# Modulation closes in three spaced calls under the down projections, and four whole tiles in place of five in the first FFN

## Chip, core and metric

The kernel runs on one core of one Trainium2 chip. The metric is the device time of one execution in microseconds (us); the time before is the median of three runs. Traces come from one profiled execution. Engines are TensorE (PE, its weight loads PEld), VectorE (DVE), ScalarE (ACT), GpSimd (POOL) and SyncE (SP, which only issues transfers).

## What is computed

One layer of a diffusion backbone: 512 latent tokens (LAT) and 256 context tokens (CX), width 1024, FFN width 2816 = 22 tiles of 128.

```python
ml = split(silu(c)     @ w_mod + b_mod, 9)      # nine modulation vectors of 1024, latent
mc = split(silu(c_ctx) @ w_mod + b_mod, 9)      # the same for the context tokens
lat += 0.5 * ml[2] * swiglu(modulate(rms_norm(lat, g0), ml[0], ml[1]), w_gu[0], w_down[0])
cx  += 0.5 * mc[2] * swiglu(modulate(rms_norm(cx,  g0), mc[0], mc[1]), w_gu[0], w_down[0])
h_lat, h_ctx = modulate(rms_norm(lat, g1), ml[3], ml[4]), modulate(rms_norm(cx, g1), mc[3], mc[4])
lat += ml[5] * merge(diff_attn(h_lat, h_ctx), pool_mix(h_lat))
lat += 0.5 * ml[8] * swiglu(modulate(rms_norm(lat, g2), ml[6], ml[7]), w_gu[1], w_down[1])
out = rms_norm(lat, g_final)
```

Everything is float32. A product of two float32 matrices is made of three TensorE matmuls on split operands (`mm3`, L141: hi*hi, lo*hi, hi*lo).

## The kernel before

**Order.** The program is written in one order; a planner that estimates times puts each engine's instructions into a queue of its own, which the chip then runs strictly in that order. `tc.issue_after(x)` keeps an instruction behind `x` in the queue of the engine that both share.

**First FFN, up and gate.** The 768 tokens are two streams of 384. The first five of the 22 tiles (`PLAIN1 = 5`) are whole tiles (`Hidden`, L373): gate and up, 8 k-tiles, two streams, 3 matmuls each = 96 matmuls of 384 columns. The other 17 are made by `Quad` (L426): seven products of 4 k-tiles from sums of weight and activation halves, 7 x 4 x 3 = 84 matmuls of 384 columns, for which DVE, ACT and POOL form and split more operands. The sums of activation halves (`HalfSums.build`, L514, four of them) are put behind the products of the third, fourth and fifth whole tile (L709 to L716). A quad's weights are prepared one quad ahead. Results go to DRAM (`store_act`, L656).

**First FFN, down.** The stored tiles come back (`Stored`, L533: a transfer, two ACT copies, two DVE subtractions) in chunks of 2, 5, 8, 3 and 4 (`ACT_CHUNKS`). A chunk is eight groups `i` of `ffn_down` (L549), each n x 6 matmuls and an update of `xo` and `xc` (L571) on DVE. The tiles of the next chunk are loaded meanwhile. The last chunk runs three times: context tokens (weight parts on POOL), then two halves of the latent tokens, with norms between its groups.

**Modulations 2 to 8** (`Mod`, L239) are work that runs beside this. A modulation has eight steps (L245: a 512 KB transfer issued by POOL into `wm`, then one DVE instruction on `macc` for each stream; 2 to 4 have two streams, 5 to 8 one) and a close: `total` (L257: TensorE matmuls that add `macc` over the partitions, L263, then an ACT copy, L266) and `finish` (L268: four small matmuls on that copy, L272, and one DVE addition, L275). Modulations 0 and 1 are made at the start in another way. Modulations 2, 3, 4 hang on the quads: each quad after the first calls `next_pending` twice (L489, L494). Modulations 5 to 8 hang on the down groups: `MOD_STEPS` says how many items each group of chunks 0 to 3 takes (L802). In the list `pending` (L724) a close is two more items behind the eight steps, so a call that takes three items can hold the last step, `total` and `finish` together. What is left runs behind chunk 3 (L804), then `scale_vec(7)` and `gate_vec(8)`.

Of the kernel before, what the change touches and what calls it, by code (L numbers as in the profile page):

```python
# [17 lines left out]
AF = mybir.ActivationFunctionType  # L18
# [6 lines left out]
KT = D // P  # L25
SEQ = 512
CTX = 256
# [8 lines left out]
CHUNKS = (4, 4, 4, 4, 2, 4)  # L36
ACT_CHUNKS = (2, 5, 8, 3, 4)

MOD_STEPS = (0, 1, 3, 2)

PLAIN1 = 5

PLAIN = 4
PARTS = 4
# [58 lines left out]
def tile_layer(ctx: ExitStack, tc: tile.TileContext, a: dict, out: bass.AP):  # L103
    nc = tc.nc
# [8 lines left out]
    latest = {}  # L113
    dr = ctx.enter_context(tc.tile_pool(name="dr", bufs=1, space=bass.MemoryType.DRAM))

    LAT, CX = 0, 1
# [13 lines left out]
    def weights(src, lo_engine=None):  # L130

        _, k, n = src.shape
        raw = wts.tile([P, 1024], F32, name="w_raw", bufs=3)
        hi = wts.tile([P, 1024], F32R, name="w_hi")
        lo = wts.tile([P, 1024], F32R, name="w_lo")
        v = lambda t: t[:, 0:k * n].rearrange("p (k n) -> p k n", n=n)
        nc.sync.dma_start(out=v(raw), in_=src)
        split(hi[:, 0:k * n], lo[:, 0:k * n], raw[:, 0:k * n], lo_engine)
        return v(hi), v(lo)

    def mm3(outs, wh, wl, acts, start, stop):  # L141

        for o, (ah, al) in zip(outs, acts):
            nc.tensor.matmul(out=o, lhsT=wh, rhs=ah, start=start, stop=False)  # L144
            nc.tensor.matmul(out=o, lhsT=wh, rhs=al, start=False, stop=False)  # L145
        for o, (ah, al) in zip(outs, acts):
            latest["pe"] = nc.tensor.matmul(out=o, lhsT=wl, rhs=ah, start=False, stop=stop)  # L147
        return sum(o.shape[-1] for o in outs) * 3 / 2400.0
# [23 lines left out]
    def bank(n=512):  # L172
        t = psum["ring"].tile([P, 512], F32, name="ps")
        return t[:, 0:n]

    def table(func, after):

        nc.scalar.activation(out=dummy, in_=after[:, 0:1], func=func, scale=0.0, bias=eps)
# [102 lines left out]
    def mod(i, kt, s):  # L281
        return mods[:, 8 * i + kt, s:s + 1]

    def scale_vec(i, norm, kts=range(KT), ns=2):

        n = len(kts)
        t = mods[:, 8 * i + kts[0]:8 * i + kts[0] + n, 0:ns]
        g = vecs[:, gn_col + 8 * norm + kts[0]:gn_col + 8 * norm + kts[0] + n]
        nc.vector.scalar_tensor_tensor(out=t, in0=t, scalar=1.0, in1=g.unsqueeze(2).broadcast_to([P, n, ns]),
                                       op0=ALU.add, op1=ALU.mult)  # L290

    def gate_vec(i, ns=2):

        t = mods[:, 8 * i:8 * i + 8, 0:ns]
        nc.vector.tensor_scalar(out=t, in0=t, scalar1=0.5, scalar2=None, op0=ALU.mult)
# [253 lines left out]
    def ffn_down(w_down, j0, acts, spans, after=no_after, held=None, lo_engine=None):  # L549

        n = len(acts)
        held = {} if held is None else held
        for i in range(KT):
            i0 = i - i % 2 if n <= 4 else i
            ws = slice((i - i0) * P, (i - i0 + 1) * P)
            if i0 not in held:
                cols = slice(0, 2 * P) if n <= 4 else slice(i % 2 * P, (i % 2 + 1) * P)  # L560
                held[i0] = weights(w_down[i0 // 2, 0, :, j0:j0 + n, cols], lo_engine)
            wh, wl = held[i0]
            outs = [bank(s[1]) for s in spans]
            for k in range(n):
                mm3(outs, wh[:, k, ws], wl[:, k, ws],
                    [acts[k].parts(o, m) if isinstance(acts[k], Stored) else
                     (acts[k].hi[:, o:o + m], acts[k].lo[:, o:o + m]) for o, m, *_ in spans],
                    k == 0, k == n - 1)
            for po, (o, m, xs, x0, gate_i, s) in zip(outs, spans):
                xa = xs[i][:, x0:x0 + m]  # L570
                latest["dve"] = nc.vector.scalar_tensor_tensor(out=xa, in0=po, scalar=mod(gate_i, i, s), in1=xa,  # L571
                                                               op0=ALU.mult, op1=ALU.add)
                after(i, s, x0, xa)
            yield i

    def run(gen, inserts=None):

        for i in gen:
            if inserts and i in inserts:
                inserts[i]()  # L580
# [34 lines left out]
    xc = [xc_all[:, k, :] for k in range(KT)]  # L615
# [34 lines left out]
    w_gu1, w_dn1 = a["gu"][0], a["dn"][0]  # L650
# [5 lines left out]
    def store_act(j, gate):  # L656
        nc.gpsimd.dma_start(out=act_dram[j], in_=gate)

    first = [Hidden(w_gu1, j, None, both, store_act) for j in range(PLAIN1)]
    early = [(first[0], 0), (first[0], 1), (first[1], 0)]  # L660
# [38 lines left out]
    sums1 = HalfSums(hb, HALF, tq1, row, nc.vector)  # L699
    quads1 = {j: Quad(w_gu1, j, wq1, 2, cq1, sums1, row, lambda q, gate: store_act(q.j, gate)) for j in range(PLAIN1, NJ)}  # L700
    for j, qd in quads1.items():
# [13 lines left out]
                    sums1.build(k)  # L715
        h_.close()  # L716

    pending = []
    behind = {}

    def add_mods(idx, pool_):
        for i in idx:
            m = Mod(i, pool_, (LAT, CX) if i < 5 else (LAT,))
            pending.extend([lambda m=m, kt=kt: m.step(kt) for kt in range(KT)] + [m.total, m.finish])  # L724

    def next_pending(n=1):

        for _ in range(min(n, len(pending))):
            with ExitStack() as order:
                for ins in (behind.get("dve"), latest["pe"]):  # L730
                    if ins is not None:
                        order.enter_context(tc.issue_after(ins.ins))
                pending.pop(0)()
        behind["dve"] = latest["dve"]

    add_mods((2, 3, 4), modp1)
    stored = []
    for j, qd in quads1.items():
        qd.all(next_pending if j > PLAIN1 else None)
        if not pending and not stored:  # L740
            right_stack.close()
            act_a = pool("act_a", right_stack, bufs=ACT_CHUNKS[0], side="right")
            raw_a = pool("raw_a", right_stack, bufs=1, side="right")
            for n in range(ACT_CHUNKS[0]):
                t = act_a.tile([P, 2, ALL], F32R, name="act_a")
                stored.append(Stored(act_dram[n], raw_a, t[:, :, 0:SEQ], t[:, :, SEQ:ALL]))
# [10 lines left out]
    def stream_tile():  # L757
        t = xo.tile([P, KT, SEQ], F32, name="xo")
        return t, [t[:, k, :] for k in range(KT)]
# [5 lines left out]
    xc = [xc_all[:, k, :] for k in range(KT)]  # L765
# [4 lines left out]
    rawp = pool("rawp", ffn_stack, bufs=2)  # L770
    modp = pool("modp", ffn_stack, bufs=2)
    add_mods((5, 6, 7, 8), modp)
    hctx_stack = ExitStack()
    HCW = CTX + 8
# [4 lines left out]
    def bring(j0, n, own):  # L779

        got = []
        for k in range(n):
            if own:
                t = actp.tile([P, 2, ALL], F32R, name="act")
                lt, ct = t[:, :, 0:SEQ], t[:, :, SEQ:ALL]
            else:
                lt = hp.tile([P, 2, SEQ], F32R, name=f"hl{k}")
                ct = hcp.tile([P, 2, HCW], F32R, name=f"hc{k}")[:, :, 0:CTX]
            got.append(Stored(act_dram[j0 + k], rawp, lt, ct))
        return got  # L790
# [3 lines left out]
    acts = stored  # L794
    for c, n in enumerate(ACT_CHUNKS[:-1]):
        nj = ACT_CHUNKS[c + 1]
        if c == 1:

            right_stack.close()
            hcp = pool("hcp", hctx_stack, bufs=1, side="right")  # L800
        following = bring(starts[c + 1], nj, c + 1 != 2)
        run(ffn_down(w_dn1, starts[c], acts, every), {i: lambda c=c: next_pending(MOD_STEPS[c]) for i in range(KT)})  # L802
        acts = following
    while pending:  # L804
        next_pending()
    scale_vec(7, 2, ns=1)
    gate_vec(8, 1)
    nc.sync.dma_start(out=edge, in_=a["edge"])
    lambdas()
    hl, hc = hl_new(), hc_new()  # L810
    st, held, j0 = Stats(), {}, starts[-1]
    run(ffn_down(w_dn1, j0, acts, [(SEQ, CTX, xc, 0, 2, CX)], st, held, nc.gpsimd), {1: lambda: table(AF.Sqrt, st.acc[CX, 0])})
    run(ffn_down(w_dn1, j0, acts, [(0, 256, xl, 0, 2, LAT)], st, held),
        Norm(st.acc[CX, 0], xc, 0, CX, 4, 3, hc).inserts(1))
    run(ffn_down(w_dn1, j0, acts, [(256, 256, xl, 256, 2, LAT)], st, held),
# [109 lines left out]
    _, o_raw = stream_tile()  # L925
# [271 lines left out]
    st = Stats()  # L1197
# [165 lines left out]
```

## Time and profile before

| | us |
|---|---|
| median of three runs | 1470.77 (1470.31 to 1474.37) |
| the profiled execution | 1472.54 |
| its span, first to last instruction | 1470.7 |
| TensorE busy | 1423.0 (97%) |
| VectorE busy | 1083.2 (74%) |
| ScalarE busy | 643.6 (44%) |
| GpSimd busy | 407.4 (28%) |

The span is cut by the program into: start and whole tiles (0 to about 117 us), quads (to about 370), down projection of the first FFN (to about 580), attention (to about 915), merge and second FFN. A line number in a row is that of the helper that issues the instruction. "PEclk" is the granted TensorE clock as a share of 2.4 GHz; 0.50 is 1.2 GHz.

### The profile page before, as it was taken

The page shows a single profiled execution, that of the slowest core. Times are in us where ns is not written, and L with a number is a line of the kernel's source. Part 1 is how long each engine was busy: PE and PEld are TensorE (multiplying, and loading weights), DVE is VectorE, ACT ScalarE, POOL GpSimd, SP SyncE. Part 2 cuts the span into 40 slices and gives each one's busy share as a digit, 9 for nine tenths or more (in the row PEclk, how much of TensorE's full clock was granted, in tenths as well). Part 3 has the DMA queues.
Part 4 walks back from the last instruction along what each step waited for, and adds up shares of the span by engine and source line. Part 5 has one row for each costly group of instructions (what it writes and reads, how often), then busy time and mean ns, then how long its engine had stood idle before and what let it go on. Part 6 is the DMA issues. An engine that isn't in the chain of part 4 may idle for free.

```text
span 1470.7 us, 22771 instructions
## 1 busy us (share of the span) xinstructions
PE 1423.0 (97%) x9076; PEld 1312.0 (89%) x9076; DVE 1083.2 (74%) x1613; ACT 643.6 (44%) x1034; POOL 407.4 (28%) x319
## 2 busy tenths in 40 slices
PE   6999999999989989989999999999999999999997
PEld 4999999999878879889999988888899898989997
DVE  5596999997785548677767676633487987878886
ACT  5342333333332126566666665422266443534343
POOL 1021323332011133545454563000144322211200
PEclk9999999999999989999999999999999999999999
DMA  9422444443896532301010111432353223323231
GB/s 376 153 87 94 153 160 152 160 145 110 292 298 196 194 104 86 102 30 57 30 59 29 58 51 51 143 101 92 112 176 116 95 96 109 105 85 115 87 101 58
DMA packets 63450, 177.14 MB, mean 120 GB/s; under 512 B 6000, under 2 KB 19568, under 8 KB 62960
## 3 DMA queue, kind: packets, MB, share of 16 engines
q1 hardware_dynamic: 52800, 136.56, 28.3%
q0 software_dynamic: 9824, 38.02, 7.6%
q8 instruction: 71, 1.16, 0.3%
q10 hardware_dynamic: 720, 1.11, 0.2%
q14 instruction: 35, 0.29, 0.1%
HBM read 162.82 MB, written 12.85 MB: 119 GB/s over the span
## 4 chain that ended last, share of the span: by engine, by line
PE 81%; DVE 9%; DMA 4%; ACT 3%; issue 2%; POOL 1%; DVEq 0%; SPq 0%; ACTq 0%; POOLq 0%
PE ps L144 24%; PE ps L145 24%; PE ps L147 24%; DMA act_raw<-act 3%; PE sc L995 1%; PE sc L994 1%; PE ps L1019 1%; PE ps L903 1%; PE ps L904 1%; PE ps L905 1%; DVE w_lo L128 1%; DVE tmp L326 1%; ACT w_hi L127 1%; DVE tmp L304 1%; DVE e L1005 1%
## 5 line engine op out<-in xcount | busy, mean ns | idle before, releaser
L127 ACT ACTIVATE w_hi<-w_raw 128x1024 fp32r<-128x1024 f32 (+3 forms) x217 | 203.3, 939 | 331.8 <-PE ps L145 308.5
L128 DVE TENSOR_TENSOR w_lo<-w_raw,w_hi 128x1024 fp32r<-128x1024 f32 (+3 forms) x179 | 202.2, 1131 | 53.7 <-ACT w_hi L127 52.8
L144 PE MATMUL ps<-hl,w_hi 128*128 128x512 f32 (+1 forms) x592 | 210.8, 359 | 0.7 <-DVE xo L1031 0.4
L145 PE MATMUL ps<-hl,w_hi 128*128 128x512 f32 (+1 forms) x592 | 209.1, 355 | 0.0
L147 PE MATMUL ps<-hl,w_lo 128*128 128x512 f32 (+1 forms) x592 | 208.5, 355 | 0.0
L128 POOL TENSOR_TENSOR w_lo<-w_raw,w_hi 128x1024 fp32r<-128x1024 f32 x38 | 93.6, 2466 | 255.1 <-ACT w_hi L127 224.3
L127 ACT ACTIVATE wq_hi<-s 128x1024 fp32r<-128x1024 f32 x70 | 73.8, 1060 | 145.0 <-PE ps L145 115.4
L458 POOL TENSOR_TENSOR s<-s,w_raw 128x512 f32<-128x512 f32 x35 | 57.4, 1639 | 264.3 <-DVE wq_lo L128 141.5
L144 PE MATMUL ps<-t,wq_hi 128*128 128x384 f32 (+1 forms) x420 | 129.7, 309 | 0.0
L145 PE MATMUL ps<-t,wq_hi 128*128 128x384 f32 (+1 forms) x420 | 129.4, 308 | 0.0
L147 PE MATMUL ps<-t,wq_lo 128*128 128x384 f32 (+1 forms) x420 | 128.8, 308 | 0.0
L144 PEld LDWEIGHTS ps<-hl,w_hi 128*128 128x128 f32 x592 | 112.1, 190 | 15.5 <-issue 0.8
L147 PEld LDWEIGHTS ps<-hl,w_lo 128*128 128x128 f32 x592 | 111.9, 190 | 12.7 <-issue 0.2
L145 PEld LDWEIGHTS ps<-hl,w_hi 128*128 128x128 f32 x592 | 112.3, 190 | 10.9
L253 DVE SCALAR_TENSOR_TENSOR macc<-wm,cond,macc 128x1024 f32<-128x1024 f32 x70 | 95.6, 1389 | 14.7 <-DMA wm<-in_wm 14.7
L571 DVE SCALAR_TENSOR_TENSOR xo<-ps,mods,xo 128x512 f32<-128x512 f32 (+1 forms) x104 | 68.1, 663 | 47.9 <-PE ps L147 46.8
L247 POOL DMA_DIRECT2D wm<-in_wm x56 | 30.1, 538 | 257.2 <-DVE macc L253 161.9
L128 DVE TENSOR_TENSOR wq_lo<-s,wq_hi 128x1024 fp32r<-128x1024 f32 x70 | 94.9, 1355 | 6.8 <-ACT wq_hi L127 6.1
L145 PE MATMUL ps<-hb,w_hi 128*128 128x384 f32 x296 | 99.3, 336 | 0.0
L144 PE MATMUL ps<-hb,w_hi 128*128 128x384 f32 x296 | 98.0, 338 | 0.6 <-ACT hb L332 0.6
L147 PE MATMUL ps<-hb,w_lo 128*128 128x384 f32 x296 | 89.2, 335 | 0.0
L1000 ACT ACTIVATE e<-sc,st 128x768 f32<-128x768 f32 x64 | 57.7, 902 | 57.8 <-DVE st L998 56.8
(297 smaller groups left out, 4022.0 us busy)
## 6 DMA issues: line engine op xcount, KB each, us to landing
w_raw<-in_gu SPq DMA_DIRECT2D x88, 512.0 KB, 3.5
wm<-in_wm POOLq DMA_DIRECT2D x56, 512.0 KB, 4.5
w_raw<-in_wi SPq DMA_DIRECT2D x36, 512.0 KB, 3.4
w_raw<-in_dn SPq DMA_DIRECT2D x32, 512.0 KB, 4.5
act<-gate POOLq DMA_DIRECT2D x22, 384.0 KB, 4.6
act_raw<-act SPq DMA_DIRECT2D x22, 384.0 KB, 5.1
wm<-in_wm SPq DMA_DIRECT2D x16, 512.0 KB, 10.8
w_raw<-in_wo SPq DMA_DIRECT2D x16, 512.0 KB, 3.5
```

The costliest lines, as they stand in the source:

```text
L127: nc.scalar.activation(out=hi, in_=src, func=AF.Copy)
L128: (lo_engine or nc.vector).tensor_tensor(out=lo, in0=src, in1=f32(hi), op=ALU.subtract)
L144: nc.tensor.matmul(out=o, lhsT=wh, rhs=ah, start=start, stop=False)
L145: nc.tensor.matmul(out=o, lhsT=wh, rhs=al, start=False, stop=False)
L147: latest["pe"] = nc.tensor.matmul(out=o, lhsT=wl, rhs=ah, start=False, stop=stop)
L247: nc.gpsimd.dma_start(out=wm, in_=a["wm"][self.i - 2, kt // 2, :, kt % 2])
L253: nc.vector.scalar_tensor_tensor(out=acc, in0=wm, scalar=c, in1=acc, op0=ALU.mult, op1=ALU.add)
L304: nc.vector.tensor_tensor(out=acc, in0=acc, in1=sq, op=ALU.add)
L326: nc.vector.scalar_tensor_tensor(out=t, in0=x, scalar=scale, in1=r, op0=ALU.mult, op1=ALU.mult)
L458: nc.gpsimd.tensor_tensor(out=s24[:, a], in0=s13[:, a], in1=g[:, a], op=ALU.add)
L571: latest["dve"] = nc.vector.scalar_tensor_tensor(out=xa, in0=po, scalar=mod(gate_i, i, s), in1=xa, op0=ALU.mult, op1=ALU.add)
L1000: nc.scalar.activation(out=ec, in_=s, func=AF.Exp, bias=mx, accum_out=st[:, 2 + c:3 + c])
```

## The change

Four whole tiles instead of five: tile 4 becomes a quad, the four `build` calls lie behind the two parts of the third and fourth tile, and `next_pending` is called from quad 5 on instead of quad 6. `pending` now holds steps only. A modulation whose last step was issued goes to a second list, `closing`: the next call makes its `total`, the call after that its `finish`. A call that makes the `total` of a two-stream modulation takes no step. `MOD_STEPS` goes from 0, 1, 3, 2 to 0, 1, 2, 1 items per group, now all steps. The close of modulation 8 moves into the context run of the last chunk (`total` behind group 2, `finish` behind group 3), and `scale_vec(7)` and `gate_vec(8)` behind that run.

```diff
-MOD_STEPS = (0, 1, 3, 2)
-PLAIN1 = 5
+MOD_STEPS = (0, 1, 2, 1)
+PLAIN1 = 4
...
-    pending = []
-    behind = {}
+    pending, closing, behind = [], [], {}
...
-            pending.extend([lambda m=m, kt=kt: m.step(kt) for kt in range(KT)] + [m.total, m.finish])
+            pending.extend((m, kt) for kt in range(KT))
 
     def next_pending(n=1):
-        for _ in range(min(n, len(pending))):
-            with ExitStack() as order:
-                for ins in (behind.get("dve"), latest["pe"]):
-                    if ins is not None:
-                        order.enter_context(tc.issue_after(ins.ins))
-                pending.pop(0)()
+        due, closing[:] = list(closing), []
+        with tc.issue_after(latest["pe"].ins):
+            for m, place in due:
+                if place:
+                    m.finish()
+                else:
+                    m.total()
+                    closing.append((m, True))
+        if any(not place and len(m.streams) == 2 for m, place in due):
+            n = 0
+        with tc.issue_after(behind["dve"].ins) if behind else ExitStack():
+            for m, kt in pending[:n]:
+                m.step(kt)
+                if kt == KT - 1:
+                    closing.append((m, False))
+        pending[:n] = []
         behind["dve"] = latest["dve"]
...
-        if not pending and not stored:
+        if not pending and not closing and not stored:
...
-    while pending:
-        next_pending()
-    scale_vec(7, 2, ns=1)
-    gate_vec(8, 1)
+    assert not pending
...
-    run(ffn_down(w_dn1, j0, acts, [(SEQ, CTX, xc, 0, 2, CX)], st, held, nc.gpsimd), {1: lambda: table(AF.Sqrt, st.acc[CX, 0])})
+    run(ffn_down(w_dn1, j0, acts, [(SEQ, CTX, xc, 0, 2, CX)], st, held, nc.gpsimd),
+        {1: lambda: table(AF.Sqrt, st.acc[CX, 0]), 2: lambda: next_pending(0), 3: lambda: next_pending(0)})
+    assert not closing
+    scale_vec(7, 2, ns=1)
+    gate_vec(8, 1)
```

## Rows read from the trace of the kernel before

**Rows 1.** Waits of PE: engine, line, what it waited for; us in total, times, longest.

```profile
PE ps L272 <- ACT tmp L266: 6.4, 3, 5.4
PE acc L263 <- DVE macc L253: 6.2, 1, 6.2
```

**Rows 2.** Timeline, close of modulation 5: start, us, engine, line, [idle before it].

```profile
436.69 0.64 PE L263 MATMUL acc<-macc,half 128*32 128x256 f32 x8
...
441.43 0.94 ACT L127 ACTIVATE act<-act_raw 128x512 fp32r<-128x512 f32 x2 [2.98 <-DMA act_raw<-act]
442.27 0.36 ACT L266 ACTIVATE tmp<-acc 128x256 f32<-128x256 f32 x1
...
442.69 1.02 PE L272 MATMUL ps<-ident,tmp 128*128 128x4 f32 x4 [5.35 <-ACT tmp L266]
```

**Rows 3.** Timeline, close of modulation 8.

```profile
525.53 1.28 DVE L253 SCALAR_TENSOR_TENSOR macc<-wm,cond,macc 128x1024 f32<-128x1024 f32 x1 [2.16 <-DMA wm<-in_wm]
526.87 1.08 PE L263 MATMUL acc<-macc,half 128*32 128x256 f32 x8 [6.19 <-DVE macc L253]
...
528.46 1.02 PE L272 MATMUL ps<-ident,tmp 128*128 128x4 f32 x4 [0.50 <-ACT tmp L266]
```

**Rows 4.** PE by stretch, behind both closes: length, busy, PEclk, DMA share, GB/s.

```profile
442.70:448.80 6.10, 6.10 (x20) 0.50 1.00 326
526.90:534.20 7.30, 6.80 (x27) 0.51 0.11 36
```

**Rows 5.** Timeline: `finish` of modulation 6 (one call) and of 7 (two calls).

```profile
472.48 0.61 PE L272 MATMUL ps<-ident,tmp 128*128 128x4 f32 x4 [0.50 <-ACT tmp L266]
...
507.45 0.51 PE L272 MATMUL ps<-ident,tmp 128*128 128x4 f32 x4
```

**Rows 6.** Timeline of the quads on PE: consecutive matmuls, and two totals.

```profile
195.12 0.33 PE L144 MATMUL ps<-hb,wq_hi 128*128 128x384 f32 x1
...
195.29 0.33 PE L145 MATMUL ps<-hb,wq_hi 128*128 128x384 f32 x1
...
195.73 1.09 PE L263 MATMUL acc<-macc,half 128*32 128x256 f32 x16
...
270.55 1.09 PE L263 MATMUL acc<-macc,half 128*32 128x256 f32 x16
```

**Rows 7.** Between these totals: all engines (PE, PEld, DVE, ACT, POOL); L253 alone; L255 alone.

```profile
195.80:270.60 74.80, 74.80 (x446) 74.01 (x448) 72.73 (x91) 25.42 (x31) 24.08 (x23) 1.00 0.48 154
...
195.80:270.60 74.80, 19.38 (x14) 1.00 0.48 154
...
195.80:270.60 74.80, 1.41 (x2) 1.00 0.48 154
```

**Rows 8.** Timeline of DVE, last split of a `build`, and the last whole tile's close.

```profile
104.15 1.95 DVE L128 TENSOR_TENSOR t<-gate,t 128x768 fp32r<-128x768 f32 x2
...
116.69 1.02 DVE L409 TENSOR_TENSOR gate<-gate,ps 128x384 f32<-128x384 f32 x2 [6.24 <-PE ps L147]
```

**Rows 9.** Timeline, context run of the last chunk: updates by DVE, ACT, POOL.

```profile
547.30 0.48 DVE L571 SCALAR_TENSOR_TENSOR xc<-ps,mods,xc 128x256 f32<-128x256 f32 x1 [0.96 <-PE ps L147]
...
548.74 0.48 DVE L571 SCALAR_TENSOR_TENSOR xc<-ps,mods,xc 128x256 f32<-128x256 f32 x1
...
548.25 1.28 ACT L178 ACT_TABLE_LOAD   x1
549.54 0.29 ACT L178 ACTIVATE dummy<-tmp,eps 128x1 f32<-128x1 f32 x1
...
538.94 2.40 POOL L128 TENSOR_TENSOR w_lo<-w_raw,w_hi 128x1024 fp32r<-128x1024 f32 x1 [14.42 <-ACT w_hi L127]
```

**Rows 10.** The page's DMA issues: transfers of `wm` by POOL, KB each, us to landing.

```profile
wm<-in_wm POOLq DMA_DIRECT2D x56, 512.0 KB, 4.5
```

**Rows 11.** Timeline of DVE, the same weight part in two quads.

```profile
194.14 1.76 DVE L128 TENSOR_TENSOR w_lo<-w_raw,w_hi 128x512 fp32r<-128x512 f32 x1
...
223.15 0.69 DVE L128 TENSOR_TENSOR w_lo<-w_raw,w_hi 128x512 fp32r<-128x512 f32 x1
```

## The prediction

> **What bounds the kernel now.** First the page's busy shares: TensorE is at 97% of the span, so time can come only from fewer matmuls, from gaps in its work, or from stretches at a lower clock. Then the list of what TensorE waited for [rows 1]: two of its largest waits belong to the close of a modulation, 6.4 us for the ACT copy L266 and 6.2 us for the DVE step L253. The timeline shows where they fall. In the close of modulation 5, `total` runs at 436.69, `finish` only at 442.69 [rows 2]: the ACT copy between them stood in ACT's queue behind a split of a stored tile, which waited for its transfer. In the close of modulation 8, `total` waited 6.19 us for the last step, whose transfer had only just landed, and `finish` 0.50 us more for the copy [rows 3]. Last, the granted clock: behind both waits TensorE ran at 0.50 and 0.51 of 2.4 GHz, its 1.2 GHz level, through 6.10 and 6.80 us of work [rows 4]. In the quads the picture is another one: TensorE 74.80 of 74.80 us, DVE 72.73 [rows 7]. There DVE is the engine to watch.
>
> **The change part by part.**
>
> *Tile 4 as a quad.* 96 matmuls become 84. Consecutive ones start 0.17 us apart (195.12, 195.29) [rows 6], so 12 x 0.173 = 2.1 us less on TensorE. What pays for it is DVE, ACT and POOL work of one more quad.
>
> *Close of modulation 5.* `total` comes behind group 0 of chunk 2, as before, `finish` now one group later. A group of the context run (4 tiles, 256 columns) takes 548.74 - 547.30 = 1.44 us [rows 9]; a group of chunk 2 has 8 tiles and 768 columns, by estimate 1.44 x 2 x 3 = 8.6 us. The wait to be hidden was 5.35 us [rows 2]. So it goes, and with it the low clock: 6.10 us at half speed are 3.05 us lost [rows 4]. Together 8.4 us. If ACT takes the copy only behind the next stored tile, a few us later, part of the wait comes back.
>
> *Close of modulation 6.* It was one call and waited 0.50 us [rows 5]; now two calls, four tiles of work apart at least: 0.5 us. Modulation 7, whose `total` and `finish` already lay a group apart, shows no wait at all [rows 5]: that is how the others should look.
>
> *Close of modulation 8.* Before, chunk 3 took two steps per group, and the close stood right behind the last one. Now one step per group, the last behind group 7 in the program, though its DVE order allows it from the update of group 6 on; `total` follows group 2 of the context run. Gone are 6.19 + 0.50 us of waiting [rows 3] and half of 6.80 us at 1.2 GHz, 3.4 us [rows 4]: 10.1 us. Is the new place late enough? A chunk 3 group is 3/4 x 3 x 1.44 = 3.2 us by the same estimate. Two `wm` buffers take turns, so a step needs the one two before it to end, a transfer of 4.5 us to land [rows 10], and 1.28 us on DVE [rows 3]: 5.8 us per two steps against 6.4 us per two groups. POOL issues these transfers between the weight parts of the last chunk, 2.40 us each [rows 9]; one of them ahead of the last transfer delays it by that much. From the update of group 6 to `total` there are 3.2 + 3 x 1.44 = 7.5 us. That covers one such delay, hardly two: 0 to 4 us, and I take 0.5, near the uncontended row.
>
> *`finish` of modulation 8.* Only one context group, 1.44 us, lies between it and `total`; the ACT copy of 0.36 us [rows 2] stands there beside squares and the load of the square-root table, 1.28 us, whose first use follows 0.01 us behind its end [rows 9]. Below zero is excluded, since the matmuls are the same; above, it is one table load plus a square, 1.7 us. I take 0.5. The Trainium skill ("ScalarE: Activation LUTs", What ACT_TABLE_LOAD costs) adds a drain of some 1.38 us to each change of set; by it this wait would be 1.4 us longer. The row shows no such drain behind the load, so the measurement decides.
>
> *Where nothing is paid.* The steps of modulation 5 to 7 are the same DVE instructions and POOL transfers, at most two per group of 8.6 us instead of three; POOL and the DMA queues get slack. Modulations 2 to 4 have 24 steps and 3 calls for `total` alone, and the last `finish` is call 28; before, 30 items. Starting a quad earlier, they end with quad 18 instead of 20, so the first two stored tiles are fetched two quads earlier. SP then has those two transfers in front of weights of the last quads; with one raw buffer the second can hold up SP until the first is split. A quad's weights come one quad ahead, which hides that; without that cover it costs up to the 2.98 us that a stored tile was waited for in [rows 2].
>
> *DVE in the quads.* Here the change adds work. A modulation took 10 calls, five quads; now 9 calls, 4.5 quads. A quad is 84 x 0.173 = 14.5 us on TensorE; two totals lie 74.82 us apart [rows 6], which leaves 2.1 us for one close and its changes of weights. DVE: 72.73 - 19.38 - 1.41 = 51.9 us in five quads without steps, 10.4 per quad [rows 7]. For 4.5 quads: 46.7 + 20.8 = 67.5 us on DVE against 4.5 x 14.5 + 2.1 = 67.4 on TensorE. So DVE goes from 97% to full. What hides a lag is that weights are made a quad ahead and that seven PSUM banks stand between the engines; three quads without steps at the end make it up. Bounds: 0, and 5 us if each of the three periods leaves 1.7 us of DVE waits over. I take 0.5, near zero, because TensorE shows no wait at 97%.
>
> *The first quad.* Its fourth product needs the sums of activation halves. In the trace their last split ends at 106.1, and DVE was let into the last whole tile's close at 116.7 by TensorE [rows 8]. The fourth tile thus ended 96 x 0.173 = 16.6 us before, at 100.1, and the first quad's first three products, 2.1 us each, would end at 106.4. That fits by little; the weight parts of the dropped tile are out of DVE's way. Bounds 0 and 4; I take 0.5.
>
> **The sum.** 2.1 + 8.4 + 0.5 + 10.1 = 21.1 us off; 2.0 back (0.5 four times): 19.1. The profiled execution, 1472.54 us, would take 1453.4. That execution is 1.8 us above the median of the runs shown, so in their measure 1470.8 - 19.1 = 1451.7.
>
> **The rivals.**
>
> *A. One wait stays.* The copy of modulation 5 again behind a stored tile, or the last `wm` transfer behind two weight parts: a wait of 4 to 6 us with its low clock, 8 to 10 of the 21 us. For it: both waits were made by transfers that came later than planned, and the order is again a plan. Against: between 7 and 9 us now lie where nothing lay. Time: 1451.7 + 8.5 = about 1460.
>
> *B. The first quad waits for its sums*, 2 to 5 us, and eats what the dropped tile gave: 1454 to 1457. For it: the margin of 0.3 us above. Against: less DVE work in front of it.
>
> *C. DVE becomes the bound of the quads, and the kernel is slower.* The place is the stretch from quad 5 to 18. It decides from the point where DVE needs 21.1 / 14 = 1.5 us more per quad than TensorE, 16.0 us instead of 15.0. For it: the same weight part took 0.69 us in one quad and 1.76 in another [rows 11], so DVE's own times can grow where POOL is at work. The Trainium skill ("GPSIMD Engine Reference", Key points) says that GpSimd shares its SBUF interfaces with VectorE and contends with instructions that have two SBUF inputs; by that rule a fuller DVE would meet POOL more often. Against: POOL's work per quad is the same, and the trace's own 10.4 us already hold such meetings. Time: for 2 us per quad too much, 14 x 2 = 28 us back, 1479.
>
> *D. The change doesn't do what it says*: the planner puts `finish` or `total` where it waits as long as before. Then only the 2.1 us are left, 1468.7.
>
> **How the numbers follow.** Forecast 0.56, A 0.20, B 0.08, C 0.06, D 0.06, and 0.04 for what I don't see. The forecast alone spans 1449.5 (all 21.1 us) to 1455 (costs at their middle). The range takes in B and A: 1449 to 1462, leaving some 0.17 outside. A difference of 0.3%, 4.4 us, is about what a measurement of this kernel can tell from none. Faster by more: forecast, A, B and half the rest, 0.86. Within: D and a mild C, 0.08. Slower: 0.06.
>
> **What would show it.** In the profile after, the waits of TensorE lack L272 on L266 and L263 on L253, or hold them under 1 us; PEclk is 1.00 all through the first FFN's down projection, where 13 us now stand at half. The quads' first total comes a quad and some 2 us earlier, and DVE is at 98% or more there while TensorE stays at 100%. I am wrong if TensorE shows a wait on DVE's `wq_lo` or on L484 in the quads (C), at the first product on `t` (B), or if a close shows a wait of over 3 us with 0.50 behind it (A, D).

## The result and the profile after

The changed kernel took 1453.68 us (median of 4, 1453.07 to 1457.08), the kernel before 1471.85 us on the same chip (1470.31 to 1474.37): a ratio of 0.9883 [0.9871, 0.9895], 18.2 us less. The forecast was 19.1 us less, 1451.7 in a range of 1449 to 1462. The profiled execution took 1453.27 us, its span is 1451.5 us. Up to the down projection the lines keep their numbers; in attention they moved by 13 (the scores are L1007 and L1008 now, before L994 and L995).

The page of after, its busy shares:

```profile
PE 1416.5 (98%) x9064; PEld 1307.0 (90%) x9064; DVE 1092.8 (75%) x1623; ACT 644.5 (44%) x1036; POOL 415.3 (29%) x321
```

What PE waited for in after (us in total, times, longest):

```profile
PE ps L642 <- POOL sq L639: 13.3, 1, 13.3
PE sc L1007 <- ACT q L904: 4.1, 1, 4.1
...
PE ps L147 <- DVE w_lo L128: 1.9, 1, 1.9
```

The two rows of [rows 1] are gone altogether: no wait on the copy L266, none on the step L253. One that was 1.6 us before stands in second place now: the first scores of attention wait 4.1 us for `q`.

Timeline of after, the close of modulation 5, PE and then ACT (start, us, idle before in brackets):

```profile
434.81 0.64 PE L263 MATMUL acc<-macc,half 128*32 128x256 f32 x8
...
443.89 0.50 PE L272 MATMUL ps<-ident,tmp 128*128 128x4 f32 x4
...
438.21 0.94 ACT L127 ACTIVATE act<-act_raw 128x512 fp32r<-128x512 f32 x2 [2.59 <-DMA act_raw<-act]
439.06 0.36 ACT L266 ACTIVATE tmp<-acc 128x256 f32<-128x256 f32 x1
```

The copy is as late as in [rows 2]: `total` ended at 435.45, and it ran at 439.06, 3.6 us later, behind a split that had waited 2.59 us for its transfer. But `finish` now comes only at 443.89, and the 8.4 us between hold the matmuls of a group.

Timeline of after, the close of modulation 8, DVE, PE and ACT:

```profile
522.94 1.29 DVE L253 SCALAR_TENSOR_TENSOR macc<-wm,cond,macc 128x1024 f32<-128x1024 f32 x1
...
526.90 0.64 PE L263 MATMUL acc<-macc,half 128*32 128x256 f32 x8
529.00 0.51 PE L272 MATMUL ps<-ident,tmp 128*128 128x4 f32 x4
...
526.54 1.28 ACT L178 ACT_TABLE_LOAD   x1
527.83 0.29 ACT L178 ACTIVATE dummy<-tmp,eps 128x1 f32<-128x1 f32 x1
...
528.34 0.37 ACT L266 ACTIVATE tmp<-acc 128x256 f32<-128x256 f32 x1
```

The last step ended at 524.23, 2.67 us ahead of `total`; the copy, behind the table load, ended at 528.71, 0.29 us ahead of `finish`.

Stretches of after: length, busy time of PE, PEld, DVE, ACT and POOL, then PEclk, DMA share and GB/s; first the down projection, then the quads up to the totals of modulations 2, 3 and 4:

```profile
434.00:445.00 11.00, 11.00 (x70) 9.14 (x69) 8.78 (x13) 3.56 (x8) 1.05 (x2) 1.00 0.99 327
...
500.00:530.00 30.00, 30.00 (x195) 26.63 (x196) 23.43 (x37) 9.33 (x14) 12.91 (x9) 1.00 0.60 195
...
117.50:179.30 61.80, 61.80 (x360) 61.55 (x359) 59.69 (x71) 21.38 (x26) 20.66 (x20) 1.00 0.48 154
179.30:243.30 64.00, 64.00 (x381) 63.24 (x380) 61.89 (x76) 21.63 (x26) 20.07 (x20) 1.00 0.50 164
243.30:313.70 70.40, 70.40 (x419) 69.57 (x418) 68.55 (x85) 23.88 (x30) 23.15 (x22) 1.00 0.46 149
```

The granted clock is 1.00 (2.4 GHz) in both stretches of the down projection, where [rows 4] show 0.50 and 0.51. TensorE never stands still in the quads, with DVE at 97%.

Where the 18 us came from shows best at four marks of TensorE that both traces have: the total of modulation 5, the last wait on L304 ahead of attention (L318), the wait on `w_lo` in the second FFN (L147), and the last wait on `xg`. Their starts were, before and after: 436.69 and 434.81; 591.26 and 570.72; 1166.07 and 1146.75; 1462.91 and 1443.62. So the first stretch gave 1.88 us, the second, with the closes of modulations 5 to 8, 154.57 - 135.91 = 18.66, the third took 576.03 - 574.81 = 1.22 back, and the last is the same (296.84 and 296.87).

The second stretch on TensorE, before and then after (length, busy, PEclk, DMA share, GB/s):

```profile
436.69:591.26 154.57, 139.28 (x894) 0.94 0.46 153
```

```profile
434.81:570.72 135.91, 133.18 (x893) 1.00 0.51 172
```

Its idle time fell from 15.29 to 2.73 us, by 12.56, and its busy time, for the same matmuls, by 6.10: the waits, and the low clock behind them. In the third stretch idle time is the same (10.39 and 10.44), and busy time rose by 1.17 us (564.42 to 565.59).

### The profile page after: what moved, and what is told of

Its sections match the earlier page's. It is cut to its first block, busy times and chain, and to the rows that moved or that the text cites. A ratio compares the mean times of both kernels' runs of the same rounds, so it can differ in the third digit from the quotient of the medians.

```text
span 1451.5 us, 22763 instructions
## 1 busy us (share of the span) xinstructions
PE 1416.5 (98%) x9064; PEld 1307.0 (90%) x9064; DVE 1092.8 (75%) x1623; ACT 644.5 (44%) x1036; POOL 415.3 (29%) x321
## 4 chain that ended last, share of the span: by engine, by line
PE 87%; DVE 7%; ACT 2%; issue 2%; POOL 1%; DMA 0%; DVEq 0%; SPq 0%; ACTq 0%; POOLq 0%
PE ps L144 26%; PE ps L145 26%; PE ps L147 26%; PE sc L1008 1%; PE sc L1007 1%; PE ps L1032 1%; PE ps L916 1%; PE ps L917 1%; PE ps L918 1%; DVE e L1018 1%; DVE w_lo L128 1%; DVE tmp L326 1%; DVE tmp L304 1%; PE acc L224 1%; ACT w_hi L127 1%
## 5 line engine op out<-in xcount | busy, mean ns | idle before, releaser
L147 PE MATMUL ps<-hl,w_lo 128*128 128x512 f32 (+1 forms) x592 | 208.2, 354 | 0.0
L144 PE MATMUL ps<-t,wq_hi 128*128 128x384 f32 (+1 forms) x432 | 133.9, 310 | 0.0
L145 PE MATMUL ps<-t,wq_hi 128*128 128x384 f32 (+1 forms) x432 | 133.3, 309 | 0.0
L147 PE MATMUL ps<-t,wq_lo 128*128 128x384 f32 (+1 forms) x432 | 133.1, 309 | 0.0
L147 PEld LDWEIGHTS ps<-hl,w_lo 128*128 128x128 f32 x592 | 111.7, 189 | 12.6 <-issue 0.2
L253 DVE SCALAR_TENSOR_TENSOR macc<-wm,cond,macc 128x1024 f32<-128x1024 f32 x70 | 98.2, 1426 | 7.5 <-DMA wm<-in_wm 7.3
L145 PE MATMUL ps<-hb,w_hi 128*128 128x384 f32 x272 | 91.3, 336 | 0.0
L144 PE MATMUL ps<-hb,w_hi 128*128 128x384 f32 x272 | 89.9, 338 | 0.1
L147 PE MATMUL ps<-hb,w_lo 128*128 128x384 f32 x272 | 83.7, 336 | 0.0
```

Source lines behind the costliest of these rows:

```text
L253: nc.vector.scalar_tensor_tensor(out=acc, in0=wm, scalar=c, in1=acc, op0=ALU.mult, op1=ALU.add)
```

## The experiments

Each kernel was timed beside the kernel before on the same chip, and its ratio is to that. Differences to the changed kernel are between medians; the four marks above, read from each trace, tell where a difference lies.

**The fourth quad alone** (e1_tile: the kernel before with four whole tiles).

```diff
-PLAIN1 = 5
+PLAIN1 = 4
```

> The kernel before with one edit: four whole tiles in place of five (PLAIN1 = 4); the closes are as before. Theory: the twelve matmuls saved are on the path, nothing waits in the quads, so 2.1 us less than before, 1469.8, with both waits (L272 on L266, L263 on L253) where they were. Rival (DVE is full, the first quad waits for its sums): the gain is eaten, 1471 to 1474, and the trace shows a wait of TensorE on the sums t or on wq_lo between 100 and 370 us.

1468.98 us, 0.9981 [0.9972, 0.999]: 2.9 us less than the 1471.9 of the kernel before. The size is near what was expected, its place is not. At the total of modulation 5 it is only 0.40 us ahead (436.29). The rest, 2.98 us, came between there and L318, where the wait for the copy was 3.74 us instead of 5.35. PE in the closes of modulations 5 and 8:

```profile
440.67 0.61 PE L272 MATMUL ps<-ident,tmp 128*128 128x4 f32 x4 [3.74 <-ACT tmp L266]
...
523.85 1.08 PE L263 MATMUL acc<-macc,half 128*32 128x256 f32 x8 [6.42 <-DVE macc L253]
```

Both waits stay, so the spacing is what took them away.

**The closes alone** (e2_closes: the changed kernel with five whole tiles).

```diff
-PLAIN1 = 4
+PLAIN1 = 5
```

> The kernel after with one edit: five whole tiles again (PLAIN1 = 5); the closes are in spaced calls as in the kernel after. Theory: both waits and both stretches at 1.2 GHz are gone without the tile, 18.9 us off what before takes and up to 1.5 us given back at the start of the attention, 1453 to 1455. Rival (tile and closes help each other): less than 15 us off, above 1457, with a wait left at a close.

1458.37 us, 0.9915 [0.9901, 0.9928], 13.5 us less than before and 3 to 5 more than I had expected. The stretch with the closes is not the reason: from the total of modulation 5 to L318 it takes 135.91 us, to the hundredth what the changed kernel takes. It is 3.10 us late when it enters that stretch (the tile's 12 matmuls are 2.1 of it, and 0.75 is a wait at 389.24 that the changed kernel hasn't), loses 0.52 us more up to the second FFN, and 1.56 us at a low clock there (last section). So the closes are worth 18.66 us in the stretch where they lie, with five whole tiles or four. But alone they also lose: against the kernel before, this one is 1.22 us later at the total of modulation 5, takes 1.74 more from L318 to the second FFN and 1.59 more in it. By time the rival's range came in (less than 15 us off, above 1457), by the profile not: no wait is left at a close. And the tile is worth between 0.40 us (e1_tile) and 3.10 (here) at that mark.

**Total and finish in one call** (e3_joint: the changed kernel, modulations 5 to 8).

```diff
-                    closing.append((m, True))
+                    if len(m.streams) == 1:
+                        m.finish()
+                    else:
+                        closing.append((m, True))
```

> The kernel after with one edit: for modulations 5 to 8, total and finish are made in the same call again, behind the same group as total is now; the steps keep their wide spacing. Theory (the distance between total and finish is what hides the ACT copy): the close of modulation 5 waits again for the copy behind a stored tile, about 4 to 5 us and 3 us at 1.2 GHz; the other three wait 0.5 us each, modulation 8 up to 1.7: 8.5 to 10.5 us more than after, 1462 to 1464. Rival (wider steps did it): at most 2 us more, 1455.

1462.05 us, 0.9936 [0.9922, 0.995], 8.4 us more than the changed kernel. The stretch up to L318 takes 144.24 us, 8.33 more: four waits on the copy, 3.26 + 0.50 + 0.50 + 1.20 = 5.5 us, and the low clock behind them. PE and ACT at modulation 5, and two stretches behind it:

```profile
440.33 1.01 PE L272 MATMUL ps<-ident,tmp 128*128 128x4 f32 x4 [3.26 <-ACT tmp L266]
...
439.07 0.94 ACT L127 ACTIVATE act<-act_raw 128x512 fp32r<-128x512 f32 x2 [1.82 <-DMA act_raw<-act]
439.91 0.36 ACT L266 ACTIVATE tmp<-acc 128x256 f32<-128x256 f32 x1
...
440.30:443.00 2.70, 2.67 (x9) 2.44 (x10) 2.70 (x6) 0.94 (x2) 0.53 (x1) 0.50 0.85 222
443.00:447.00 4.00, 4.00 (x16) 3.40 (x15) 0.15 (x1) 0.00 (x0) 0.00 (x0) 0.63 1.05 367
```

**The steps as dense as before** (e4_dense: the changed kernel with the old `MOD_STEPS`).

```diff
-MOD_STEPS = (0, 1, 2, 1)
+MOD_STEPS = (0, 1, 3, 2)
```

> The kernel after with one edit: the steps of before, MOD_STEPS = (0, 1, 3, 2), so that all 32 are called by the end of chunk 2; the closes stay in spaced calls, that of modulation 8 then behind groups 0 and 1 of chunk 3. Theory (the last transfer needs time before total): three steps per group of 8.4 us against 5.8 us per two steps from two buffers, 8.7, so the steps fall behind and the last one is not done when total comes 3.2 us later: a wait of 1 to 4 us at L263, with the low clock if it is long, 1455 to 1460. Rival (spaced closes alone are enough): no wait, 1453 to 1454.

1465.32 us, 0.996 [0.9947, 0.9973], 11.6 us more than the changed kernel, twice what I had expected at most. PE at modulation 8's total, its last step on DVE, and PE behind it:

```profile
507.71 1.08 PE L263 MATMUL acc<-macc,half 128*32 128x256 f32 x8 [5.37 <-DVE macc L253]
...
506.28 1.28 DVE L253 SCALAR_TENSOR_TENSOR macc<-wm,cond,macc 128x1024 f32<-128x1024 f32 x1 [2.77 <-DMA wm<-in_wm]
...
507.70:511.00 3.30, 3.29 (x15) 2.21 (x16) 2.98 (x7) 1.67 (x2) 0.00 (x0) 0.50 0.18 22
511.00:515.00 4.00, 4.00 (x23) 3.50 (x22) 0.40 (x2) 0.00 (x0) 0.00 (x0) 0.85 0.40 150
```

`total` behind a step whose transfer has only just landed waits nearly as long as in [rows 3], although it is a call of its own. The stretch up to L318 takes 7.46 us more (143.37). The other 4 us are not of the closes: it is 1.80 us late at modulation 5, and loses 0.99 up to the second FFN and 1.54 in it. So modulation 5 needs `finish` spaced from `total`, and modulation 8 needs `total` spaced from its last step.

**The price of the clock** (e5_cover: e3_joint with 15 matmuls on old data between total and finish of modulation 5; they add work).

```diff
+                    if m.i == 5:
+                        t = spare["act"]
+                        o = bank()
+                        for _ in range(15):
+                            latest["pe"] = nc.tensor.matmul(out=o, lhsT=t[:, 0, 0:P], rhs=t[:, 0, :], start=True, stop=True)
...
+        spare["act"] = acts[0].lat
```

> The kernel with total and finish of modulations 5 to 8 in one call (1462.05 us), with 15 matmuls on old data put between total and finish of modulation 5; they add work and change no result. There TensorE waited 3.26 us for the copy and then ran 2.70 us at a granted clock of 0.50 and 4.00 us at 0.63. Theory (a wait costs itself and the low clock behind it): the 15 matmuls at about 0.22 us fill the 3.3 us, and the clock stays at 1.00 behind them, which gives back 2.70 x 0.50 + 4.00 x 0.37 = 2.8 us: 1459.2. Rival (the clock falls there for another reason, or what is saved is waited for later): the clock stays low, and the time is 1462 or a little more.

1458.93 us, 0.9913 [0.9898, 0.9928]: 3.1 us less than e3_joint, though the matmuls add 3.5 us of work. The stretch up to L318 went from 144.24 to 141.76 us, 2.48 less, where 2.8 were expected; the three small waits of 0.5, 0.5 and 1.2 us stay. PEclk behind the close is whole:

```profile
440.00:443.00 3.00, 3.00 (x19) 2.59 (x19) 1.42 (x4) 0.72 (x2) 0.53 (x1) 1.00 0.83 259
443.00:447.00 4.00, 4.00 (x25) 3.46 (x24) 1.03 (x2) 0.94 (x2) 0.00 (x0) 1.00 0.81 314
```

So here the low clock comes with the idle time and not with the place, and the wait of 3.26 us costs some 2.5 us more in the work behind it: the same time, filled with useless matmuls, is cheaper than left empty.

**How much room modulation 8 has** (e6_early8: total behind group 0 of the context run instead of group 2).

```diff
-        {1: lambda: table(AF.Sqrt, st.acc[CX, 0]), 2: lambda: next_pending(0), 3: lambda: next_pending(0)})
+        {1: lambda: table(AF.Sqrt, st.acc[CX, 0]), 0: lambda: next_pending(0), 2: lambda: next_pending(0)})
```

> The changed kernel with total of modulation 8 behind group 0 of the context run instead of group 2, and finish behind group 2. In the changed kernel the last step of modulation 8 ended at 524.2 and total began at 526.90: a margin of 2.7 us. Total now comes two groups, 2.9 us, sooner. Theory (the place just suffices, so that the margin is the 2.7 us of the trace): a wait of 0 to 0.6 us on L253 and no more; finish no longer close behind the table load; time 1453 to 1455. Rival (the last step follows its place in the order and not its transfer, or it is later in most runs): a wait of 2 us or more with a low clock behind it, 1456 to 1459.

1455.38 us, 0.9887 [0.9872, 0.9902]; no wait at a close. DVE's last step and PE:

```profile
522.97 1.27 DVE L253 SCALAR_TENSOR_TENSOR macc<-wm,cond,macc 128x1024 f32<-128x1024 f32 x1
...
524.61 0.64 PE L263 MATMUL acc<-macc,half 128*32 128x256 f32 x8
```

The step ended at 524.24, 0.37 us ahead of `total`. The room was as large as the trace said, and up to L318 it is worth nothing (135.91 us again). The median is 1.7 us higher than the changed kernel's; of the 2.0 us between the two traces, 1.57 are the low clock in the second FFN, 298.44 us instead of 296.87 behind the mark there.

**One whole tile fewer** (e7_three: the changed kernel with three, two builds under each half of the third).

```diff
-PLAIN1 = 4
+PLAIN1 = 3
...
-            k = 2 * n + part
-            if k < HK:
+            for k in (2 * part, 2 * part + 1):
```

> The changed kernel with three whole tiles instead of four: both builds of a part are put under the third one. TensorE loses 12 more matmuls, 2.1 us. Theory (the first quad had no room left, its sums are the limit): a build takes DVE about 7 us (in the changed kernel 92 to 99 with the weights), two in a part of 8.3 us don't fit, the fourth product waits some 6 to 10 us for t, and the time is 1456 to 1462. Rival (room is left, because DVE can build ahead): a wait under 1 us and 1451.5 to 1452.5.

1461.95 us, 0.9931 [0.9916, 0.9946], 8.3 us more than the changed kernel. PE at the first quad's fourth product, and a stretch behind its first waits:

```profile
91.42 0.45 PE L144 MATMUL ps<-t,wq_hi 128*128 128x384 f32 x1 [0.59 <-ACT t L127]
93.89 0.44 PE L145 MATMUL ps<-t,wq_hi 128*128 128x384 f32 x1 [2.02 <-DVE t L128]
...
97.44 0.69 PE L144 MATMUL ps<-t,wq_hi 128*128 128x384 f32 x1 [2.93 <-ACT t L127]
99.45 0.69 PE L145 MATMUL ps<-t,wq_hi 128*128 128x384 f32 x1 [1.33 <-DVE t L128]
...
96.00:101.00 5.00, 2.23 (x6) 1.81 (x7) 5.00 (x6) 3.26 (x5) 4.46 (x2) 0.50 0.00 0
```

As the theory had it: 6.87 us of waiting for `t`, with DVE full (5.00 of 5.00 us), and the low clock behind. This is rival B, one tile further on: with four whole tiles the sums are ready in time, with three not.

**What DVE has to spare in the quads** (e9_dve: one addition of each quad made five times; it adds work).

```diff
-            add(up[:, t0], u2, p7)
+            for _ in range(5):
+                add(up[:, t0], u2, p7)
```

> The changed kernel with one DVE addition of every quad (128x384 out of PSUM, 0.55 us, 0.46 us apart in a row) made five times instead of once; the result is the same. That is 1.86 us more of DVE work per quad. In the changed kernel DVE was busy 188.13 - 2.1 - 2.1 - 1.85 us while TensorE was at 100%: 190.13 of 196.20 us in the three periods, so 6.07 us were free in 13.5 quads, 0.45 per quad. Theory (DVE stands just under its limit in the quads with steps, and little of a lag is hidden): 1.86 - 0.45 = 1.41 us too much in 13.5 quads is 19 us, of which the buffers hide a few: 1467 to 1473, all of the change's gain, with waits of TensorE on DVE in the quads. Rival (half of DVE's busy time there is the stretching of its instructions by others, or there is slack that the busy share hides): under 8 us, 1454 to 1462.

(The busy time that the expectation reckons with is 190.13 us, the sum of the three rows of after; the first figure in it is a slip.) 1483.35 us, 1.0082 [1.0066, 1.0098], 29.7 us more than the changed kernel, and 10 more than the theory's upper end. What PE waited for; the three periods; one stretch behind a wait of 4.94 us:

```profile
PE ps L144 <- DVE up L484: 17.9, 7, 4.9
...
117.50:187.70 70.20, 64.93 (x357) 64.05 (x355) 67.95 (x90) 21.39 (x26) 18.32 (x20) 0.95 0.46 150
187.70:260.90 73.20, 66.51 (x382) 64.75 (x381) 69.40 (x93) 21.74 (x26) 19.80 (x20) 0.98 0.43 137
260.90:341.30 80.40, 73.77 (x417) 72.04 (x416) 79.74 (x108) 24.57 (x30) 21.19 (x22) 0.96 0.41 136
...
178.60:181.00 2.40, 2.33 (x7) 2.33 (x8) 2.37 (x4) 0.00 (x0) 1.95 (x2) 0.50 0.86 268
```

The periods take 223.8 us instead of 196.2, 27.6 more. On TensorE 18.6 of these are waits on L484 and 9.0 are busy time, 205.2 instead of 196.2, with the low clock behind the waits. On DVE they are work: its busy time rose by 27.0 us to 217.1 of 223.8, and none of its longer waits there is for TensorE. So DVE set the pace, and whether the low clock added anything is not shown. What the expectation had wrong, for the most part, is the 6.07 us that it took as free: without them 1.86 us in 13.5 quads are 25 us, not 19. DVE, now the bound, stands at 97%, the same share as in after. So 97% is here already next to full. In after its idle time is for the most part waiting for `wm`:

```profile
DVE macc L253 <- DMA wm<-in_wm: 4.1, 4, 1.7
```

**The filling ahead of attention** (e8_fill: the changed kernel with more of it; e11_fill12: more still; e10_bfill: the kernel before with as much as e8_fill). All three change one number:

```diff
-FILL_0, FILL_A, FILL_B, TAIL = 3.9, 2.8, 2.2, 2.0
+FILL_0, FILL_A, FILL_B, TAIL = 8.0, 2.8, 2.2, 2.0
```

> The changed kernel with 8.0 us of planned filling ahead of the first scores of attention instead of 3.9. There TensorE waited 4.12 us for q and then ran from 603.5 to 608 at 0.50 to 0.72, and its lead on the kernel before shrank from 20.5 to 19.3 us. Theory (the wait and the clock behind it ate the 1.2 us, and products that are moved ahead of the scores take their place without a new wait): 1449 to 1452. Rival (the filling is only taken from later stretches, where its lack makes as long a wait): 1453 to 1455.

> The changed kernel with 12.0 us of planned filling ahead of the first scores; with 8.0 us it took 1451.09 us, and 0.74 and 0.33 us of waiting were left there. Theory (with the wait gone there is nothing more to win): 1450 to 1452. Rival (the filling is taken from the last head, where 1.61 us of waiting came up with 8.0 us): 1452.5 to 1455.

> The kernel before with 8.0 us of planned filling ahead of attention's first scores instead of 3.9. It waited 1.64 us there (the changed kernel 4.12 us, behind 11 filling matmuls fewer), and 4.80 us more in the first head. Theory (the changed kernel's loss there is the missing filling, which the kernel before had; filling more repairs what came with the change): the kernel before wins the 1.64 us at most, 1470 to 1472. Rival (the start of attention has the same waits in both, and the filling is an edit of its own that has nothing to do with the change): as much as in the changed kernel, 2.6 us or more, below 1469.3.

First what the change had done there. PE's filling matmuls from L318 to the first scores, before (591.2 to 624.0) and then after (570.7 to 603.5): count, busy us, mean ns:

```profile
L145 PE MATMUL ps<-hl,w_hi 128*128 128x512 f32 x24 | 9.4, 390 | 0.0
L144 PE MATMUL ps<-hl,w_hi 128*128 128x512 f32 x24 | 9.1, 391 | 0.0
...
L147 PE MATMUL ps<-hl,w_lo 128*128 128x512 f32 x23 | 8.8, 391 | 0.0
```

```profile
L145 PE MATMUL ps<-hl,w_hi 128*128 128x512 f32 x20 | 7.8, 391 | 0.0
L147 PE MATMUL ps<-hl,w_lo 128*128 128x512 f32 x20 | 7.7, 391 | 0.0
L144 PE MATMUL ps<-hl,w_hi 128*128 128x512 f32 x20 | 7.5, 392 | 0.0
```

What PE waited for at the first scores in the kernel before:

```profile
PE sc L994 <- ACT q L891: 1.6, 1, 1.6
```

71 filling matmuls became 60. Eleven fewer, 0.23 us apart, are 2.5 us, and the wait for `q` grew from 1.64 to 4.12 us, by 2.5. The scores came no later for it (32.83 and 32.82 us behind the mark at L318), but the work left undone is done later, and the clock falls: of the 1.22 us of this stretch 1.17 are busy time. Stretches of after at the first scores:

```profile
603.00:605.00 2.00, 1.46 (x5) 1.36 (x6) 1.24 (x2) 1.95 (x4) 0.00 (x0) 0.68 0.00 0
605.00:607.00 2.00, 2.00 (x7) 1.71 (x6) 1.43 (x3) 0.44 (x2) 0.00 (x0) 0.50 0.00 0
```

With 8.0 us, PE at the first scores (a second wait there is 0.33 us):

```profile
603.77 0.45 PE L1007 MATMUL sc<-k,q 128*128 128x384 f32 x1 [0.74 <-ACT q L904]
```

1451.09 us (1450.26 to 1451.73), 0.9858 [0.9842, 0.9875], 2.6 us less than the changed kernel: of the kernels run here the fastest. L318 to the second FFN takes 573.24 us, 2.79 less. With 12.0 it is 1452.96 us, 0.9871 [0.9857, 0.9884], and 573.91, which is what the rival had: the waits come back at the end of attention (3.26 us on L1018 at 884.92, where e8_fill has 1.61). The kernel before with 8.0 took 1470.83 us, 0.9993 [0.9984, 1.0002]: by time no gain clear of the noise, as the theory had it. By its trace the same stretch went from 574.81 to 572.90, 1.91 us less, while the second FFN lost 1.6 us to its clock in that execution. So by these single traces some two thirds of what the filling gives (1.91 of 2.79) was to be had before the change as well; the rest, 0.9 us, is near the 1.22 that the change gave back. That the planner fills less there belongs to where the closes lie: with them in one call (e3_joint) 71 filling matmuls ran up to the scores, and the stretch took 574.68 us. Why its plan turns out so, these runs don't show.

## Why the prediction was right

**The sum of the closes.** 8.4 + 0.5 + 10.1 = 19.0 us was forecast, and 18.66 came: 12.56 of idle time, where the four waits make 12.54, and 6.10 of busy time, where half of the low-clock time in [rows 4] makes 6.45. The mechanism is the forecast's, step by step: the copy stayed late and a group covered it (e3_joint takes the cover away, and the wait returns); modulation 8's last transfer needed room, and had it (e4_dense, e6_early8). The way the clock was priced held as well: e5_cover gave 2.5 us back for 2.8 reckoned.

**The tile.** 2.1 us forecast, 1.88 at modulation 5's total. Added alone it gave 0.40 there (e1_tile), taken away alone it cost 3.10 (e2_closes): waits of 0.3 to 0.75 us come and go in the first FFN with each change of order, and e3_joint and e4_dense, which have the same tiles as the changed kernel, come 1.62 and 1.80 us later to the same mark. So this term is known to 1 or 2 us only.

**The four reserves of 0.5 us** were hardly needed. `total` of modulation 8 had 2.7 us to spare, `finish` 0.29; the first quad and the quads show no wait. Of these two margins that of `finish` is the narrower. The Trainium skill ("ScalarE: Activation LUTs", What ACT_TABLE_LOAD costs) adds a drain of some 1.38 us to each change of table set. The trace of after shows none: the ACT instruction ahead of the load ends at 526.52, the load starts at 526.54 and ends at 527.82, and its first user starts at 527.83, as in [rows 9]. The first quad had more room than the 0.3 us reckoned: its fourth product began at 106.37, as forecast, but the split that it reads last had ended at 105.07, and by the code only its tenth matmul, at 107.93, reads it.

**DVE in the quads** was mis-sized, with the right outcome. From [rows 7] I took 10.4 us per quad without steps. From modulation 2's total to modulation 4's, nine quads, after shows 61.89 + 68.55 = 130.4 us of DVE, where my figures give 2 x 67.5 = 135.0: I had divided a window by five quads that held a few instructions more. I also forecast 98% or more; it is 97%, and e9_dve shows that this is all that there is. So rival C stood nearer than I had it: in the traces of e3_joint and e4_dense, whose edits don't touch the quads, TensorE waits 1.1 and 0.2 us on `wq_lo` there, the sign named for C. I put its deciding point at 1.5 us per quad over TensorE (16.0 us against 15.0 is a slip: it should be 16.5). By e9_dve 1.86 us more on DVE per quad cost 29.7 us, so by estimate the 18.2 us would be gone at some 1.1 us more than the change puts there. The Trainium skill ("GPSIMD Engine Reference", Key points) has GpSimd share its SBUF interfaces with VectorE and contend with VectorE instructions that have two SBUF inputs. The additions of e9_dve don't test that, since one of their two inputs lies in PSUM. The steps (L253) have two in SBUF, and beside the fuller DVE they got no longer: 59.07 us for 42 of them in the three periods of after, 57.61 in e9_dve.

**What I did not foresee** is the 1.22 us that attention gave back. The sum left out that the planner's filling follows from the whole program, so that a change in the first FFN can empty a place 70 us behind it. 18.66 + 1.88 - 1.22 = 19.3 us is the difference of the two traces (1470.7 - 1451.5 = 19.2). That the medians lie 18.2 apart is within what either varies.

**What was luck.** The sum comes so near because two errors cancel. The two terms fell short by 0.34 and 0.22 us and attention took 1.22, 1.8 us in all; the 2.0 us held back for four other places, where nothing was paid, made up for it.

Rivals A, B and D did not occur; e4_dense (one wait stays, with its clock: 7.5 us in that stretch) shows that A's price of 8.5 was about right.

## What to carry to other kernels

A step that waits for another engine's short answer belongs one group of matmuls behind its question, and the question one transfer behind its last operand; both spacings have to be there, and each has to cover the queue of the engine that answers, not the operation alone. Price a wait of TensorE with the low clock behind it, where the clock fell in these runs 0.4 to 0.9 of the wait's own length. Behind a change that speeds one stage up, look whether a planner still fills the next stage's first wait.

## What the runs showed of the hardware

In the second FFN the kernels listed below wait 1.7 to 1.9 us once for `w_lo` (L147). In some profiled executions the clock falls behind that wait, in others it does not. After, around the wait that ended at 1146.75, and e2_closes, around one of the same length that ended at 1150.37:

```profile
1145.00:1150.00 5.00, 3.25 (x14) 2.68 (x15) 4.86 (x10) 1.78 (x3) 0.00 (x0) 1.00 0.82 288
1150.00:1155.00 5.00, 5.00 (x24) 4.14 (x23) 4.90 (x7) 2.27 (x3) 0.00 (x0) 1.00 0.36 131
```

```profile
1150.00:1155.00 5.00, 4.63 (x13) 3.69 (x14) 4.76 (x10) 2.00 (x3) 0.00 (x0) 0.66 0.77 296
```

It costs 1.6 us: 298.4 us instead of 296.9 from there to the last wait in e2_closes, e3_joint, e4_dense, e6_early8 and e10_bfill, but not in before, after, e1_tile, e5_cover, e7_three, e8_fill and e11_fill12. TensorE was busy and at 1.00 ahead of the wait in both kinds, and the wait's length does not tell them apart (1.89 us without a fall in e8_fill, 1.7 with one in e3_joint). What does was not found; for differences of 1 to 2 us between kernels the marks of the traces are the better measure.
